# Output projection by pairs of units: two PSUM banks at a time, the attention's halves of both first, then the convolution's halves of both

## The chip, the cores and the metric

The kernel runs on 1 core of one Trainium2 chip. The time is device microseconds (us) of one execution of the whole program, taken from the runs of one kernel. A run of the hardware profiler gives, beside it, a span and a trace of every instruction. Engines are named as the profile does: PE is TensorE's matmul, PEld its weight load, DVE is VectorE, ACT is ScalarE, POOL is GpSimd, SP is SyncE, whose queue issues the DMAs. L213 is line 213 of the kernel; TensorE's clock has two levels, 1.2 and 2.4 GHz, which the profile gives as a granted share of 0.50 and 1.00.

## The reference

Two layers of a streaming encoder, all in fp32. A prompt of 1024 tokens and 8 samples of 16 tokens (128 together) pass through both layers; D_MODEL is 1024, the attention is 512 wide (8 heads of 64, 2 key and value heads), the convolution has 512 channels and 31 taps, the feed-forward is 4096 wide. Cut to what matters here:

```
def project(h, w_in, q_g, k_g, pos):
    q, k, v, a, b = jnp.split(h @ w_in, [...])
    ...                       # norm of q and k by head, partial rotary
    return q, k, v, a * jax.nn.sigmoid(b)

def conv_tail(u_ext, w, b, ln_g, ln_b):
    y = depthwise_conv31(u_ext, w) + b
    mu = mean(y); var = mean(square(y - mu))          # over the 512 channels
    return silu((y - mu) * rsqrt(var + EPS) * ln_g + ln_b)

def finish_layer(x, attn_o, conv_o, beta_a, beta_c, w_out, g2, w_up, w_down):
    x = x + concatenate([attn_o * beta_a, conv_o * beta_c]) @ w_out
    h = rms_norm(x, g2)
    return x + square(relu(h @ w_up)) @ w_down
```

`h @ w_in` starts from an RMS norm of x, and the attention is a sliding window over three chunks of 64 tokens with one sink logit for each head; the samples see their cached keys instead. The change touches the product with `w_out` alone.

## The kernel before, in words

**Tiling.** The 1152 tokens are three blocks (0, 1, 2) of 384 columns; the samples are the last 128 columns of block 2. Activations lie with the channels on the partitions, so a product takes a weight tile of 128 x 128 as the stationary operand and 384 columns as the moving one. An fp32 operand is kept as a rounded part and a remainder (fp32r), and a product takes three matmuls: rounded by rounded, rounded by remainder, remainder by rounded (L213, L214, L215 in `gemm`). One output tile of 128 channels over 1024 inputs, a *unit*, is 8 steps of three, 24 matmuls, into one PSUM bank.

**A weight's way.** `unit` (L195) makes two `half_unit`s of four steps each: SP issues a DMA of 256 KB into one of four buffers "raw", ACT rounds it (L205), POOL takes the remainder (L206) into one of six buffers "w". The remainder is what the third matmul of a step waits for.

**PSUM.** All products with 384 columns share three banks with the tag "g", which `pg` hands out: the input projection, the up and down projections, and `w_out`. Other banks are r (sums over channels and their spreading), c, m and s (attention). A bank is free for the next product when its result has been read, in `w_out` by DVE's addition into x (L688).

**`w_out`, L682 to L689.** For each of the 8 output tiles: a bank, a unit, whose steps 0 to 3 read the attention's result `ao` and 4 to 7 the convolution's `co`, the addition, and `unit_done` (L166), which moves the side lanes (attention, convolution, weight forms) on by a step at their rates and puts in feed-forward products of an earlier block.

**Where it is called.** `out(b)` in `run` completes the convolution's tail of block b (`tail_of`: mean, mean square at L242, the root as a power on POOL, its spreading over the partitions by PE at L248, the product with it at L663, then SiLU on ACT), loads x, calls `w_out`, and for blocks 0 and 1 the RMS norm ahead of the up projection (sum of squares L265 and L266, its root, products with it L276 and L278). It is called six times. In layer 0, block 0 comes without feed-forward products beside it, blocks 1 and 2 have them; in layer 1 all three have. Layer 1's block 0 has those of layer 0's block 2.

**What sets the order.** The program is written as a list and then set by a scheduler of the tile framework, which holds the written order as priorities and simulates the engines (`schedule_with_timeline_sim=True`, L1258). So each engine's queue follows its estimate of when operands are there, and the written order only in part; an edit in one place can move instructions elsewhere. A queue runs in its order: an instruction that waits holds all behind it.

Names in the rows: ao and co as above, hid a hidden tile of the feed-forward (L716 is the down projection, L718 its addition into x), c and u the convolution (L348, one tap of one tile of channels), pt the attention's transposed probabilities (L553 their remainder, L561 the product with the values), p and m the samples' (L612 scales them, L616 transposes them, L596 their scores), s small statistics, f and h the norm's output, vec and cst constants.

Of the kernel before, what the change touches and what calls it, by code (L numbers as in the profile page):

```python
# [11 lines left out]
ALU = mybir.AluOpType  # L12
# [8 lines left out]
KT = D // 128  # L21
UP = 30 + 256
SEG = CS + DEC_T
NS, NW, NRAW, NT, WK = 9, 6, 4, 8, 4
# [37 lines left out]
class Kernel:  # L62
# [619 lines left out]
    def w_out(self, l, x, ao, co):  # L682
        nc, a = self.nc, self.a
        h = lambda p, k: ao[:, p, k] if k < 4 else co[:, p, k - 4]
        for m in range(KT):
            ps, _ = self.pg()
            self.mark = self.gemm(ps, self.unit(a["w"][l, 14 + m]), h)
            nc.vector.tensor_tensor(out=x[:, m], in0=x[:, m], in1=ps, op=ALU.add)  # L688
            self.unit_done()  # L689


    def hidden(self, ps):
# [479 lines left out]
def _layout(i):  # L1172
# [12 lines left out]
    w = np.empty((DEPTH, 86, 128, 8, 128), np.float32)  # L1185
    w[:, :14] = tiles(w_in[:, :, cols])
    w[:, 14:22] = tiles(w_out)
    w[:, 22:54] = tiles(f("w_up"))
    w[:, 54:] = f("w_down").reshape(DEPTH, 8, 4, 128, 8, 128)[:, :, np.argsort(ROW)].transpose(0, 1, 3, 4, 2, 5).reshape(DEPTH, 32, 128, 8, 128)
# [72 lines left out]
```

## Time and profile before

| | |
|---|---|
| time, median of 3 runs | 2398.71 us (2397.44 to 2403.24) |
| profiled execution | 2401.53 us |
| its span | 2399.6 us |
| granted TensorE clock, mean | 0.991 |
| PE busy | 2319.6 us, 97% |
| PEld busy | 2257.2 us, 94% |
| DVE busy | 1652.4 us, 69% |
| POOL busy | 1533.8 us, 64% |
| ACT busy | 1270.9 us, 53% |
| DMA | 266.49 MB, 111 GB/s over the span |

The busy shares say which engine fills the span; they are means over stages with different limits. In the timeline a row is a run of like instructions of one engine: its start, its length, and in brackets the idle time of the engine just ahead of it with what ended it. Matmuls are pipelined and their ends modelled. The busy time of a matmul is the time it took, at whatever clock; the windows give the granted clock of a stretch beside it.

### The profile page before, as it was taken

Reading aid. Unit: us, or ns where it says so; the run is one execution under the profiler, and the core shown is the slowest. Engines: PE = TensorE matmul, PEld = TensorE weight load, DVE = VectorE, ACT = ScalarE, POOL = GpSimd, SP = SyncE. Lnnn points to the kernel's source line nnn. Section 1 sums busy time; section 2 is a strip of 40 time slices with the busy share of each in tenths; the row PEclk is TensorE's granted clock in tenths of the full one; section 3 lists DMA queues with packets and bytes.
Section 4 is the critical chain, followed back from the end, with each engine's and each line's share of the span. In section 5 each row is a group of like instructions: output and inputs, shape, how many; then the busy total and the mean of one; then the engine's idle time right before and its main releaser. Section 6 shows DMA issues by size and latency. Waiting matters only on the chain.

```text
span 2399.6 us, 38990 instructions
## 1 busy us (share of the span) xinstructions
PE 2319.6 (97%) x13822; PEld 2257.2 (94%) x13822; DVE 1652.4 (69%) x2997; ACT 1270.9 (53%) x2732; POOL 1533.8 (64%) x1371
## 2 busy tenths in 40 slices
PE   6899898999999999999999999999999999999999
PEld 6889898999999999999999999999999899999999
DVE  5999987996377777696687763699833877752222
ACT  5466655665335555644565476466443555544442
POOL 6875576666467666766956776856445766666662
PEclk9899899999999999999999999999999999999999
DMA  5322433333322122433333344423333122244432
GB/s 180 135 83 91 137 97 114 116 128 118 111 93 81 65 71 86 167 121 126 106 115 121 113 152 129 134 94 123 98 101 119 58 67 75 84 163 137 132 127 75
DMA packets 164259, 266.49 MB, mean 111 GB/s; under 512 B 24752, under 2 KB 55728, under 8 KB 164016
## 3 DMA queue, kind: packets, MB, share of 16 engines
q1 hardware_dynamic: 164064, 264.01, 33.6%
q8 instruction: 108, 1.77, 0.3%
q14 instruction: 87, 0.71, 0.1%
HBM read 250.19 MB, written 16.05 MB: 111 GB/s over the span
## 4 chain that ended last, share of the span: by engine, by line
PE 75%; DVE 18%; POOL 2%; DMA 2%; issue 2%; ACT 1%; SPq 0%; DVEq 0%; POOLq 0%; ACTq 0%
PE g L716 13%; PE g L213 13%; PE g L215 12%; PE g L214 12%; DVE c L348 6%; PE x L999 5%; PE x L919 4%; PE g L999 3%; PE g L919 2%; PE m L716 2%; PE r L716 2%; PE c L716 1%; POOL w L886 1%; DVE f L276 1%; DVE x L718 1%
## 5 line engine op out<-in xcount | busy, mean ns | idle before, releaser
L206 POOL TENSOR_TENSOR w<-raw,w 128x512 fp32r<-128x512 f32 x728 | 971.1, 1344 | 579.5 <-ACT w L205 562.9
L205 ACT CAST w<-raw 128x512 fp32r<-128x512 f32 x728 | 445.0, 619 | 452.0 <-PE g L716 127.3
L213 PE MATMUL g<-h,w 128*128 128x384 f32 x1696 | 577.4, 341 | 6.1 <-ACT h L277 3.5
L214 PE MATMUL g<-h,w 128*128 128x384 f32 x1696 | 574.9, 339 | 1.1 <-DVE h L278 1.1
L215 PE MATMUL g<-h,w 128*128 128x384 f32 x1696 | 575.4, 339 | 0.0
L348 DVE SCALAR_TENSOR_TENSOR c<-u,vec,c 128x384 f32<-128x384 f32 (+1 forms) x960 | 498.0, 519 | 18.6
L716 PE MATMUL g<-hid,w 128*128 128x384 f32 x2304 | 429.3, 340 | 6.7 <-DVE x L718 5.3
L716 PEld LDWEIGHTS g<-hid,w 128*128 128x128 f32 x2304 | 399.3, 189 | 15.1 <-DVE x L718 9.9
L213 PEld LDWEIGHTS g<-h,w 128*128 128x128 f32 x1696 | 322.2, 190 | 9.5 <-ACT h L277 4.3
L214 PEld LDWEIGHTS g<-h,w 128*128 128x128 f32 x1696 | 322.0, 190 | 2.9 <-DVE h L278 2.0
L215 PEld LDWEIGHTS g<-h,w 128*128 128x128 f32 x1696 | 321.8, 190 | 1.1 <-issue 0.3
L700 DVE TENSOR_TENSOR hid<-t,hid 128x384 fp32r<-128x384 f32 x128 | 106.4, 832 | 198.1 <-ACT hid L699 198.0
L886 POOL TENSOR_TENSOR w<-S,w 128x512 fp32r<-128x512 f32 x96 | 139.8, 1459 | 117.0 <-ACT w L885 116.8
L718 DVE TENSOR_TENSOR x<-x,g 128x384 f32<-128x384 f32 x240 | 129.8, 548 | 78.0 <-PE g L716 77.7
L697 ACT ACTIVATE t<-g 128x384 f32<-128x384 f32 x128 | 62.9, 492 | 144.8 <-PE g L215 143.8
L999 PE MATMUL x<-F,w 128*128 128x384 f32 x624 | 119.1, 336 | 2.9 <-DVE x L1002 2.0
L886 POOL TENSOR_TENSOR w<-raw,w 128x512 fp32r<-128x512 f32 x64 | 90.8, 1419 | 41.4 <-ACT w L885 40.1
L999 PEld LDWEIGHTS x<-F,w 128*128 128x128 f32 x624 | 109.4, 188 | 4.2 <-DVE x L1002 2.3
L999 PE MATMUL g<-F,w 128*128 128x384 f32 x528 | 108.2, 340 | 3.6 <-ACT F L808 1.5
L885 ACT CAST w<-S 128x512 fp32r<-128x512 f32 x96 | 59.7, 622 | 93.7 <-DVE S L872 48.4
L999 PEld LDWEIGHTS g<-F,w 128*128 128x128 f32 x528 | 92.6, 188 | 7.8 <-ACT F L808 2.7
L886 POOL TENSOR_TENSOR w<-A,w 128x512 fp32r<-128x512 f32 x64 | 87.0, 1364 | 17.8 <-ACT w L885 17.6
(231 smaller groups left out, 4005.6 us busy)
## 6 DMA issues: line engine op xcount, KB each, us to landing
raw<-in_w SPq DMA_DIRECT2D x792, 256.0 KB, 2.6
A<-in_w SPq DMA_DIRECT2D x64, 256.0 KB, 2.7
x<-in_x SPq DMA_DIRECT2D x24, 384.0 KB, 5.3
x<-xd SPq DMA_DIRECT2D x12, 384.0 KB, 5.4
kept<-x SPq DMA_DIRECT2D x4, 768.0 KB, 3.9
x<-kept SPq DMA_DIRECT2D x8, 384.0 KB, 4.3
xd<-x SPq DMA_DIRECT2D x4, 768.0 KB, 3.5
out_y<-x SPq DMA_DIRECT2D x4, 768.0 KB, 5.2
```

What stands on the lines that cost most here:

```text
L205: nc.scalar.copy(u[:, 0], raw)
L206: nc.gpsimd.tensor_tensor(out=u[:, 1], in0=raw, in1=u[:, 0].bitcast(F32), op=ALU.subtract)
L213: nc.tensor.matmul(ps, lhsT=u(0, k), rhs=h(0, k), start=k == 0, stop=False)
L214: nc.tensor.matmul(ps, lhsT=u(0, k), rhs=h(1, k), start=False, stop=False)
L215: self.pe = nc.tensor.matmul(ps, lhsT=u(1, k), rhs=h(0, k), start=False, stop=k == KT - 1)
L348: t = nc.vector.scalar_tensor_tensor(out=o, in0=src(k), scalar=w, in1=o, op0=ALU.mult, op1=ALU.add)
L700: nc.vector.tensor_tensor(out=hid[:, 1], in0=f, in1=hid[:, 0].bitcast(F32), op=ALU.subtract)
L716: self.pe = nc.tensor.matmul(ps, lhsT=u(p), rhs=hid[:, q], start=i == 0, stop=i == n - 1)
L718: nc.vector.tensor_tensor(out=x[:, m], in0=x[:, m], in1=ps, op=ALU.add)
L886: nc.gpsimd.tensor_tensor(out=u[:, 1], in0=f[n], in1=u[:, 0].bitcast(F32), op=ALU.subtract)
L919: nc.tensor.matmul(ps, lhsT=u[:, p, k], rhs=H[h](q, k), start=start and k == 0 and i == 0, stop=k == 3 and i == 2, skip_group_check=True)
L999: nc.tensor.matmul(o, lhsT=u[:, p, 2 * i + j], rhs=F(j, hn)[:, q], start=start and n == 0, stop=n == 5, skip_group_check=True)
```

## The change

The loop over 8 output tiles becomes a loop over 4 pairs. A pair takes two banks at once; then four half units follow: attention's of the first tile, attention's of the second, convolution's of the first, convolution's of the second. Each bank's accumulation starts with its first attention matmul and stops with its last convolution matmul, so it stays open while the other bank's half is done. Both additions and both `unit_done` come at the end of the pair. `gemm` is written out in the loop; the matmuls of the projection are now at L692, their additions at L694, and lines behind are six higher than before (L716 becomes L722).

```
--- before.py
+++ after.py
@@ -682,11 +682,17 @@
     def w_out(self, l, x, ao, co):
         nc, a = self.nc, self.a
         h = lambda p, k: ao[:, p, k] if k < 4 else co[:, p, k - 4]
-        for m in range(KT):
-            ps, _ = self.pg()
-            self.mark = self.gemm(ps, self.unit(a["w"][l, 14 + m]), h)
-            nc.vector.tensor_tensor(out=x[:, m], in0=x[:, m], in1=ps, op=ALU.add)
-            self.unit_done()
+        for m0 in range(0, KT, 2):
+            ps = [self.pg()[0] for _ in range(2)]
+            for part in range(2):
+                for i in range(2):
+                    u = self.half_unit(a["w"][l, 14 + m0 + i][:, part * WK:part * WK + WK])
+                    for k in range(WK):
+                        for j, (p, q) in enumerate(((0, 0), (0, 1), (1, 0))):
+                            self.mark = self.pe = nc.tensor.matmul(ps[i], lhsT=u[:, p, k], rhs=h(q, part * WK + k), start=part + k + j == 0, stop=part == 1 and k == WK - 1 and j == 2)
+            for i in range(2):
+                nc.vector.tensor_tensor(out=x[:, m0 + i], in0=x[:, m0 + i], in1=ps[i], op=ALU.add)
+                self.unit_done()
 
 
     def hidden(self, ps):
```

The scheduler sets all queues anew, and the places where they differ begin in the second pair of layer 0's first projection. Three of them follow.

PE, layer 0, ahead of the convolution's halves of block 1 (g is a bank, hid a down projection, ao a unit's attention half, co a convolution half, L248 the spreading of the convolution tail's root, L450 and L407 are statistics and turns of queries and keys). Before:

```order
L213 MATMUL g_4275<-ao_1778,w_4277 128x384
L214 MATMUL g_4275<-ao_1778,w_4277 128x384
L215 MATMUL g_4275<-ao_1778,w_4277 128x384
L248 MATMUL r_3919<-cst,s_3927 128x128 x3
L450 MATMUL r_3988<-cst,s_3783 64x128 x2
L407 MATMUL r_3999<-cst,t_3412 128x128
L213 MATMUL g_4030<-co_3941,w_4037 128x384
L213 MATMUL g_4117<-co_3941,w_4124 128x384
```

The first three are the last of 12 matmuls of the same attention half; ahead of those 12 stands the down projection g_4183. Now:

```order
L722 MATMUL g_4183<-hid_3565,w_4179 128x384 x3
L722 MATMUL g_4183<-hid_3671,w_4179 128x384 x3
L248 MATMUL r_3919<-cst,s_3927 128x128 x3
L692 MATMUL g_4275<-ao_1778,w_4278 128x384 x12
L450 MATMUL r_3988<-cst,s_3783 64x128 x2
L407 MATMUL r_3999<-cst,t_3412 128x128
L692 MATMUL g_4030<-co_3941,w_4067 128x384
```

L248 stood behind the 12 matmuls of the attention half, and stands ahead of them now.

DVE, layer 0, ahead of the first products of the RMS norm behind block 0's projection (L348 is a convolution step, L503, L565 and L567 belong to the attention). Before:

```order
L503 RECIPROCAL s_3050<-s_3050 128x4
L348 SCALAR_TENSOR_TENSOR c_3092<-u_1779,vec,c_3092 128x384 x2
L565 TENSOR_TENSOR og_2663<-m_2648,vec 128x256
L348 SCALAR_TENSOR_TENSOR c_3092<-u_1779,vec,c_3092 128x384
L567 TENSOR_TENSOR ao_1778<-og_2663,ao_1778 128x4x64
L276 SCALAR_TENSOR_TENSOR f_3250<-x_2764,vec,r_3231 128x384 x2
```

Now:

```order
L503 RECIPROCAL s_3085<-s_3085 128x4
L348 SCALAR_TENSOR_TENSOR c_3127<-u_1779,vec,c_3127 128x384
L565 TENSOR_TENSOR og_2663<-m_2648,vec 128x256
L348 SCALAR_TENSOR_TENSOR c_3127<-u_1779,vec,c_3127 128x384 x2
L567 TENSOR_TENSOR ao_1778<-og_2663,ao_1778 128x4x64
L348 SCALAR_TENSOR_TENSOR c_3127<-u_1779,vec,c_3127 128x384
L553 TENSOR_TENSOR pt_2874<-m_2873,pt_2874 128x512
L348 SCALAR_TENSOR_TENSOR c_3127<-u_1779,vec,c_3127 128x384 x2
L276 SCALAR_TENSOR_TENSOR f_3250<-x_2764,vec,r_3231 128x384 x2
```

A split of 512 columns (L553) came ahead of the norm's products. Counted from the first addition of squares of this norm to L276, the convolution steps are 27 in place of 25, the splits of 512 columns 3 in place of 2.

PE, layer 1, at the samples' first step (L596 scores, L616 transposes of the probabilities, g_18333 and g_18358 two down projections). Before:

```order
L716 MATMUL g_18314<-hid_18184,w_18310 128x384 x2
L596 MATMUL s_18248<-kc_17974,qb_18242 128x144 x6
L616 MATMUL m_18020<-cst,p_17999 128x128 x2
L616 MATMUL m_18020<-cst,p_18000 128x128 x2
L716 MATMUL g_18333<-hid_17968,w_18329 128x384 x3
L716 MATMUL g_18333<-hid_18088,w_18329 128x384 x3
```

Now:

```order
L722 MATMUL g_18314<-hid_18184,w_18310 128x384 x2
L596 MATMUL s_18248<-kc_17974,qb_18242 128x144 x6
L722 MATMUL g_18333<-hid_17968,w_18329 128x384 x3
L722 MATMUL g_18333<-hid_18088,w_18329 128x384 x3
L722 MATMUL g_18333<-hid_18135,w_18329 128x384 x3
L722 MATMUL g_18333<-hid_18184,w_18329 128x384 x3
L722 MATMUL g_18358<-hid_17968,w_18354 128x384 x3
L722 MATMUL g_18358<-hid_18088,w_18354 128x384 x3
L722 MATMUL g_18358<-hid_18135,w_18354 128x384 x3
L722 MATMUL g_18358<-hid_18184,w_18354 128x384 x3
L616 MATMUL m_18020<-cst,p_17999 128x128 x2
L616 MATMUL m_18020<-cst,p_18000 128x128 x2
```

Two down projections, 24 matmuls, came between the samples' scores and the transposes.

## Rows read from the trace of the kernel before

**Rows 1.** The page: span, then busy time, share and instructions of each engine.

```profile
span 2399.6 us, 38990 instructions
PE 2319.6 (97%) x13822; PEld 2257.2 (94%) x13822; DVE 1652.4 (69%) x2997; ACT 1270.9 (53%) x2732; POOL 1533.8 (64%) x1371
```

**Rows 2.** Windows: stretch, length, busy PE, PEld, DVE, ACT, POOL, clock, DMA, GB/s.

```profile
298.00:304.00 6.00, 5.99 (x19) 5.99 (x20) 6.00 (x11) 1.45 (x2) 0.69 (x1) 0.50 0.00 0
361.00:366.00 5.00, 3.04 (x25) 2.93 (x22) 3.05 (x7) 1.33 (x4) 5.00 (x5) 1.00 0.40 137
382.80:386.00 3.20, 3.20 (x10) 3.04 (x11) 3.16 (x8) 2.15 (x5) 0.97 (x1) 0.50 0.98 377
1651.00:1655.00 4.00, 2.88 (x10) 2.47 (x11) 4.00 (x9) 0.60 (x2) 3.21 (x4) 0.67 0.39 131
1800.00:1850.00 50.00, 50.00 (x289) 50.00 (x289) 22.10 (x41) 17.72 (x33) 27.34 (x22) 1.00 0.39 132
```

**Rows 3.** PE's timeline, 240 to 300: start, length, group, [idle before, releaser].

```profile
245.20 1.61 PE L561 MATMUL m<-pt,v 128*128 128x256 f32 x9 [2.12 <-DVE pt L553]
...
292.07 1.33 PE L561 MATMUL m<-pt,v 128*128 128x256 f32 x9 [0.93 <-DVE pt L553]
...
294.85 0.90 PE L248 MATMUL r<-cst,s 128*128 128x128 f32 x3 [1.44 <-POOL s L236]
...
298.01 1.01 PE L213 MATMUL g<-h,w 128*128 128x384 f32 x2 [1.41 <-ACT h L277]
```

**Rows 4.** PE's timeline, 362 to 384.

```profile
363.58 2.37 PE L716 MATMUL g<-hid,w 128*128 128x384 f32 x12 [1.97 <-DVE x L718]
...
375.23 0.41 PE L213 MATMUL g<-ao,w 128*128 128x384 f32 x1 [0.74 <-ACT w L205]
...
377.41 0.49 PE L248 MATMUL r<-cst,s 128*128 128x128 f32 x3
...
379.74 0.44 PE L450 MATMUL r<-cst,s 128*64 128x128 f32 x4 [1.85 <-DVE u L663]
...
382.78 1.33 PE L213 MATMUL g<-co,w 128*128 128x384 f32 x3 [1.88 <-ACT co L641]
```

**Rows 5.** PE's timeline in layer 1, beside its second projection.

```profile
1651.29 0.44 PE L616 MATMUL m<-cst,p 128*128 128x128 f32 x2 [0.90 <-DVE p L612]
...
1652.56 0.69 PE L616 MATMUL m<-cst,p 128*128 128x128 f32 x2 [0.83 <-DVE p L612]
```

**Rows 6.** DVE's timeline, 289 to 292.

```profile
289.10 0.68 DVE L553 TENSOR_TENSOR pt<-m,pt 128x512 fp32r<-128x512 f32 x1
...
290.34 1.28 DVE L348 SCALAR_TENSOR_TENSOR c<-u,vec,c 128x384 f32<-128x384 f32 x2
```

**Rows 7.** POOL's timeline, 290 to 295.

```profile
290.45 0.86 POOL L231 TENSOR_TENSOR s<-s,half 128x3 f32<-128x3 f32 x1
...
292.66 1.32 POOL L231 TENSOR_TENSOR s<-s,half 128x6 f32<-128x6 f32 x1
...
294.61 0.19 POOL L236 TENSOR_TENSOR s<-s,s 128x3 f32<-128x3 f32 x1
```

**Rows 8.** POOL's timeline, 368 to 375.

```profile
368.80 0.85 POOL L231 TENSOR_TENSOR s<-s,half 128x3 f32<-128x3 f32 x1
...
372.27 1.29 POOL L206 TENSOR_TENSOR w<-raw,w 128x512 fp32r<-128x512 f32 x1 [0.21 <-ACT w L205]
...
374.69 0.19 POOL L236 TENSOR_TENSOR s<-s,s 128x3 f32<-128x3 f32 x1
```

**Rows 9.** DVE's timeline, 371 to 378.

```profile
371.52 0.56 DVE L718 TENSOR_TENSOR x<-x,g 128x384 f32<-128x384 f32 x1 [4.13 <-PE g L716]
...
377.93 1.75 DVE L663 TENSOR_TENSOR u<-u,r 128x1536 f32<-128x1536 f32 x1 [2.85 <-PE r L248]
```

**Rows 10.** DVE's timeline in layer 1, ahead of the samples' transposes.

```profile
1650.40 2.10 DVE L612 TENSOR_SCALAR p<-p,s 128x256 f32<-128x256 f32 x2
```

**Rows 11.** Waits of PE: engine, line, waited for: us in total, times, longest.

```profile
PE g L716 <- DVE x L718: 5.3, 6, 2.0
```

## The prediction

> **What bounds the kernel now.** The page comes first: TensorE (PE) is busy for 2319.6 of 2399.6 us [rows 1]. So a change of order pays only where PE stands still, or runs at a lower clock. At the full clock one matmul of 384 columns costs PE 173 ns: 289 of them fill 50 us [rows 2]. Next I read PE's timeline for rows with an idle time in brackets, and then the granted clock around each. The reader is to see that idle time in the out projections is scarce. The four first places are: before the convolution's halves of block 0 in layer 0, where the longest wait is 2.12 us, and after block 0's projection, 0.93 + 1.44 + 1.41 = 3.78 us in all [rows 3]; before the convolution's halves of block 1, 1.97 + 0.74 + 1.85 + 1.88 us [rows 4]; and in layer 1 beside its second projection 0.90 + 0.83 us [rows 5]. The clock stands at 0.50 (1.2 GHz) in 298 to 304 and in 382.8 to 386, and is 0.67 on average in 1651 to 1655, each time after PE has idled [rows 2].
>
> **What the change does to the counts: nothing.** Each of the 48 units keeps 24 matmuls, two weight loads, two casts, two splits and one addition; no instruction is added or removed. What moves is the order, and with it two things: two of the three PSUM banks "g" belong to a projection at a time, and SP, ACT and POOL bring four half units as attention, attention, convolution, convolution. The scheduler then sets every queue anew, so I go by the places where the two orders differ.
>
> **Block 0's projection, layer 0: 0 at its start.** The change's plain promise, attention halves to run while the convolution is late, is already kept before: PE has the attention's halves of three units ahead of the wait at 245.20 [rows 3], one in each bank, and in the changed order also three. Up to there all queues hold the same work; the convolution's last product and its pass through ACT end the wait, as now. 0 us.
>
> **After it: +2.0 us.** The up projection at 298.01 waits for the RMS norm of this block [rows 3]. On VectorE (DVE) two more convolution steps and one split of 512 columns now stand ahead of the norm's products (counted from the first addition of squares to L276): a pair of steps takes 1.28 us, the split 0.68 us [rows 6], together 1.96 us. DVE has no idle row here, so they count in full. On POOL the key's power, 1.32 us, goes ahead of the norm's, where it stood in its midst [rows 7]. The chain on POOL starts later by DVE's shift and ends with both interleaved, so I do not add the 1.32 again: +2.0, bounds 0 (DVE has work in hand to give back) and 1.96 + 1.32 = 3.3.
>
> **Block 1's projection, layer 0: -2.8 us.** Here PE waits at 382.78 for the convolution tail, whose chain is mean square (L242), root on POOL, spreading it (L248), product (L663), SiLU on ACT. The root starts at 368.80 and its last step is over at 374.69 + 0.19 = 374.9 [rows 8], but L248 runs at 377.41 [rows 4]: in PE's queue it stands behind a unit's 12 attention matmuls, which themselves begin after a wait of 0.74. In the changed order L248 stands directly behind the last down projection, and the 12 follow it. So it can go earlier by 0.74 + 12 x 0.173 = 2.8 us; by POOL's end alone, 2.5. POOL also has one weight split less (1.29 [rows 8]) between the root's steps. The 12 matmuls then fill part of the wait that L248 to L663 causes (1.85). L663 begins at 377.93, right behind L248, and takes 1.75 [rows 9]; all behind it moves with it. The wait of 1.97 does not go: then the first down projection waited for an addition, now it follows the last query's statistics out of their bank, which DVE reads at about the same time. -2.8; bounds 0 (another link of the chain is late) and -(0.74 + 1.85 + 1.88) = -4.5.
>
> **The clock behind it: -0.8 us.** Ten matmuls fill the 3.2 us at 0.50 [rows 2], half of that is lost, 1.6. With the wait shorter, the drop may go or stay; I take half. Bounds -1.6 and +1.6 (such a drop elsewhere).
>
> **Layer 1, first sample step: -3.0 us.** PE's transposes L616 wait twice for DVE's scaled probabilities, ready at 1650.40 + 2.10 = 1652.50 [rows 5, 10]. In the changed order two down projections, 24 matmuls or 4.2 us, stand between the scores and these transposes; PE would reach them near 1654.6. DVE has two additions of at most 0.56 [rows 9] put ahead of the scaling, ready by 1653.6, still in time. So 0.90 + 0.83 go, and with the idle time the dip: (1 - 0.67) x 4 = 1.3 us. -3.0, bounds 0 and -3.0.
>
> **Elsewhere 0**: in the other projections PE is full in both orders, the feed-forward products of the background hide what moves on SP, ACT and POOL; without that cover a weight load and its cast would show.
>
> Sum: +2.0 - 2.8 - 0.8 - 3.0 = -4.6 us. Against the profiled execution's 2401.5 us (2.0 more than its span) this gives 2396.9. The median of the runs shown is 2398.7, so I forecast 2394.1. By the bounds: -9.1 to +4.9, that is 2389.6 to 2403.6.
>
> **Rivals.** *Banks run short (slower).* Five of the six projections have feed-forward products beside them, 20 pairs. If at each pair a down projection finds the only free bank still waiting for its addition, PE loses at least one addition, 0.56 us [rows 9]: 11.2 us. With +2.0 and -2.8 that is 2409. It decides from 13 pairs on (7.3 us). For it: the wait of 1.97 is of this kind [rows 4], and four down projections and a unit share one bank in the changed order ahead of block 1's convolution halves. Against it: all waits of L716 for such additions are 5.3 us in six places [rows 11], though units and down projections share the banks before too, and in most pairs both units of a pair follow each other without a product between, so the third bank is idle rather than short. Where PE did wait 1.97, the clock of 361 to 366 stayed at 1.00 (2.4 GHz) [rows 2]. The Trainium skill, "TensorE: Matmul & The Clock Gate", section "A second HAM failure mode: psum-queue depth-cycling", says that a kernel that cycles through its PSUM banks idles often enough between groups for the clock to swing between its two levels. By that rule this rival would cost more than its additions; the stretch just named does not bear it out.
>
> *The drops go (faster).* DVE gives its 2.0 back before the up projection, block 1's chain takes the whole -4.5, and both clock losses go: -4.5 - 1.6 - 3.0 = -9.1, 2389.6. For it: DVE's convolution steps done earlier are not to be done later, and PE-bound stretches follow. Against: it needs every step at its good end.
>
> *The orders are a wash.* The scheduler places instructions by its own times; where the chip differs, another link takes over. With +2.0, nothing at block 1, and only the 1.7 us of waits gone in layer 1, the time is 2399. For it: the change does not do at block 0 what it is made for, since that order was there already. Against: L248's 2.5 us behind its operand is plain in the trace.
>
> **Chances.** Forecast 0.46, wash 0.20, drops go 0.24, banks short 0.10. About 0.3% (7.2 us) can be told from no change. Faster: all of the third but its weaker part, 0.21, and the good end of the forecast, 0.06, makes 0.27. Slower: the bank rival, 0.10. The rest, 0.63, is the same. The range takes the bounds a little further on both sides, for orders that I weighed only by their waits: 2388 to 2405, which leaves out the bank rival and the far end of the fast one. The likeliest case's own range is 2390 to 2403.
>
> **What would show it.** In the changed profile: a longer wait ahead of the first up projection behind block 0's projection (about 3.3 us at near 300 for 1.41); L248 of the convolution tail right behind a down projection and near 374 to 377, and block 1's first convolution half 1 us earlier than 382.78 (2.0 late, 2.8 early); no idle row at the first L616 of layer 1 and clock 1.00 there. Many short waits of L716 or L692 for additions would make the bank rival right. Idle time at new places in 400 to 690 or 1380 to 1720 would make the forecast wrong.

## The result, and the profile after

The changed kernel takes 2416.18 us (median of 4 runs, 2414.68 to 2421.46), the kernel before in the same comparison 2399.13 us (2397.44 to 2403.24, 4 runs): ratio 1.0072, 95% interval 1.0059 to 1.0085. I had forecast 2394.1, with 2405 as the upper end: 2416, 17 us slower, is outside the range.

The page of the changed kernel, span and busy times:

```profile
span 2414.1 us, 38981 instructions
PE 2324.5 (96%) x13822; PEld 2260.7 (94%) x13822; DVE 1672.1 (69%) x2997; ACT 1271.4 (53%) x2732; POOL 1525.7 (63%) x1371
```

Against [rows 1] the span is 14.5 us longer. PE makes the same 13822 matmuls in 4.9 us more, so some of them ran at the lower clock; the other 9.6 us are idle time of PE. To find the place, I set the two timelines side by side at landmarks that both have: the mean square of block 0's convolution tail near 230 us, the first up projection behind block 0 near 298, the first product of layer 0's paired feed-forward that goes from its hidden tiles F into a bank x, near 750 (paired feed-forward: blocks 0 and 1 together, behind block 2's projection; below this landmark is "the first product with F", though a few products from F into banks g come up to 11 us earlier in both kernels), and the end.

| stretch | before | after |
|---|---|---|
| start to mean square | 231.5 | 228.3 |
| mean square to first up projection | 66.6 | 69.9 |
| up projection to first product with F | 452.7 | 464.9 |
| from there to the last matmul | 1644.9 | 1646.9 |

The first row is no effect of the change: up to there all queues are the same, and six kernels whose block 0 is as before reach this point between 228.1 and 231.7 us. Most of the loss lies in the third row, which holds the projections of blocks 1 and 2. The windows of the kernel before over that row (stretch, length, busy PE, PEld, DVE, ACT, POOL, clock, DMA, GB/s; 560 only parts the two projections):

```profile
298.00:382.80 84.80, 77.79 (x479) 73.36 (x479) 60.34 (x110) 39.71 (x76) 60.52 (x74) 0.96 0.30 97
382.80:560.00 177.20, 176.02 (x1077) 171.50 (x1078) 164.12 (x389) 109.01 (x291) 105.43 (x97) 0.99 0.38 122
560.00:708.50 148.50, 146.86 (x837) 144.09 (x836) 78.87 (x132) 62.28 (x115) 86.02 (x72) 1.00 0.33 106
708.50:750.70 42.20, 36.26 (x198) 33.69 (x197) 33.12 (x43) 25.70 (x53) 29.33 (x20) 1.00 0.26 86
```

and of the kernel after:

```profile
298.20:381.50 83.30, 78.00 (x476) 73.67 (x476) 62.74 (x107) 39.22 (x75) 59.59 (x74) 0.95 0.33 99
381.50:560.00 178.50, 172.39 (x1052) 167.45 (x1053) 165.95 (x383) 108.15 (x288) 105.42 (x98) 0.99 0.38 118
560.00:712.60 152.60, 149.17 (x844) 147.03 (x843) 78.57 (x135) 63.95 (x119) 87.52 (x73) 0.99 0.34 106
712.60:763.10 50.50, 42.66 (x215) 39.62 (x214) 35.40 (x46) 25.30 (x54) 28.40 (x20) 0.93 0.24 79
```

Length less busy PE is idle time: 7.0, 1.2, 1.6 and 5.9, together 15.8 us before; 5.3, 6.1, 3.4 and 7.8, together 22.7 after. The lower clock costs (1 - clock) x length; summed over windows of 5 us it is 4.7 us before and 10.6 after. So of the 12.3 us (464.94 less 452.66) some 6.9 are waits, and nearly as much, 5.9, is the slower clock (idle time at the lower clock counts in both). The last window also holds 17 more matmuls, 2.9 us, that stood ahead of it before.

PE's timeline of the changed kernel at these places (start, length, group, [idle before, releaser]):

```profile
298.20 1.01 PE L213 MATMUL g<-h,w 128*128 128x384 f32 x2 [2.41 <-ACT h L277]
...
362.27 0.38 PE L442 MATMUL g<-cst,t 128*128 128x2 f32 x2 [2.10 <-DVE s L439]
...
375.50 0.49 PE L248 MATMUL r<-cst,s 128*128 128x128 f32 x3
...
381.54 0.79 PE L692 MATMUL g<-co,w 128*128 128x384 f32 x3 [1.71 <-ACT co L641]
383.75 4.96 PE L692 MATMUL g<-co,w 128*128 128x384 f32 x18 [1.43 <-DVE co L642]
...
487.26 4.95 PE L722 MATMUL g<-hid,w 128*128 128x384 f32 x27 [1.52 <-DVE x L724]
...
531.08 5.48 PE L722 MATMUL g<-hid,w 128*128 128x384 f32 x30 [1.77 <-DVE x L724]
...
692.38 0.79 PE L722 MATMUL g<-hid,w 128*128 128x384 f32 x3 [1.72 <-POOL w L206]
694.23 2.08 PE L722 MATMUL g<-hid,w 128*128 128x384 f32 x7 [1.07 <-DVE x L724]
```

and the windows around the waits, where the clock is read in the column ahead of the last two:

```profile
363.70:367.20 3.50, 3.50 (x15) 3.50 (x14) 0.56 (x1) 0.58 (x1) 3.25 (x5) 0.51 0.22 74
381.60:387.00 5.40, 3.97 (x14) 3.66 (x15) 5.31 (x8) 2.09 (x5) 2.45 (x2) 0.75 0.63 230
384.20:387.70 3.50, 3.50 (x13) 3.50 (x13) 2.71 (x6) 0.00 (x0) 0.89 (x1) 0.51 0.26 85
692.00:698.00 6.00, 4.55 (x16) 4.24 (x17) 6.00 (x12) 1.88 (x4) 6.00 (x7) 0.74 0.30 101
720.00:726.00 6.00, 4.05 (x14) 3.81 (x14) 5.76 (x7) 2.18 (x4) 3.89 (x3) 0.72 0.14 44
736.00:742.00 6.00, 2.68 (x15) 2.03 (x13) 6.00 (x8) 1.43 (x3) 3.81 (x3) 1.00 0.02 6
742.00:748.00 6.00, 6.00 (x26) 6.00 (x27) 3.90 (x7) 5.30 (x13) 5.08 (x4) 0.72 0.43 131
1667.00:1671.00 4.00, 4.00 (x24) 4.00 (x25) 4.00 (x6) 1.71 (x7) 4.00 (x5) 1.00 0.47 131
```

In 736 to 742 PE stands still for 3.3 of 6 us, and in the next 6 us it is busy throughout but makes 26 matmuls where the full clock has room for 35. Between 560 and 750 us the clock of before was 1.00 throughout, so the three drops, in 692 to 698, 720 to 726 and 742 to 748, are new. The last row answers to the dip in layer 1 [rows 2, 5]: PE is full there at 1.00.

### The profile page after: what moved, and what is told of

The parts are those of the page before. It is cut to its first block, busy times and chain, and to the rows that moved or that the text cites. A ratio compares the mean times of both kernels' runs of the same rounds, so it can differ in the third digit from the quotient of the medians.

```text
span 2414.1 us, 38981 instructions
## 1 busy us (share of the span) xinstructions
PE 2324.5 (96%) x13822; PEld 2260.7 (94%) x13822; DVE 1672.1 (69%) x2997; ACT 1271.4 (53%) x2732; POOL 1525.7 (63%) x1371
## 4 chain that ended last, share of the span: by engine, by line
PE 52%; DVE 6%; POOL 1%; issue 1%; DMA 1%; ACT 0%; DVEq 0%; POOLq 0%; ACTq 0%
PE g L722 9%; PE g L213 8%; PE g L214 8%; PE g L215 8%; PE g L692 4%; PE x L1005 3%; PE x L925 2%; PE m L722 2%; PE r L722 2%; PE g L1005 2%; PE c L722 1%; PE g L925 1%; DVE c L348 1%; PE s L526 1%; POOL w L892 1%
## 5 line engine op out<-in xcount | busy, mean ns | idle before, releaser
L206 POOL TENSOR_TENSOR w<-raw,w 128x512 fp32r<-128x512 f32 x728 | 967.4, 1339 | 582.4 <-ACT w L205 553.1
L348 DVE SCALAR_TENSOR_TENSOR c<-u,vec,c 128x384 f32<-128x384 f32 (+1 forms) x960 | 498.4, 519 | 19.2
L722 PE MATMUL g<-hid,w 128*128 128x384 f32 x2304 | 431.2, 341 | 10.2 <-DVE x L724 7.4
L722 PEld LDWEIGHTS g<-hid,w 128*128 128x128 f32 x2304 | 400.7, 189 | 18.4 <-DVE x L724 11.4
L692 PE MATMUL g<-co,w 128*128 128x384 f32 x576 | 111.9, 343 | 3.5 <-ACT co L641 2.1
L692 PE MATMUL g<-ao,w 128*128 128x384 f32 x576 | 108.7, 338 | 3.2 <-DVE x L694 2.5
```

The source lines that it names most:

```text
L206: nc.gpsimd.tensor_tensor(out=u[:, 1], in0=raw, in1=u[:, 0].bitcast(F32), op=ALU.subtract)
L348: t = nc.vector.scalar_tensor_tensor(out=o, in0=src(k), scalar=w, in1=o, op0=ALU.mult, op1=ALU.add)
L692: self.mark = self.pe = nc.tensor.matmul(ps[i], lhsT=u[:, p, k], rhs=h(q, part * WK + k), start=part + k + j == 0, stop=part == 1 and k == ...
L722: self.pe = nc.tensor.matmul(ps, lhsT=u(p), rhs=hid[:, q], start=i == 0, stop=i == n - 1)
```

## The experiments

Every ratio is to the kernel before on the same chip. Beside the ratio stands the time from the mean square near 230 us to the first product with F (519.2 us before, 534.8 in the full change), since it tells where a ratio comes from. These times are from one profiled execution of each kernel.

**The place: pairs in one block only.** The edit of the first four (`w_pairs` is the projection as changed, `w_out` as before):

```
-self.w_out(l, x[b], ao[b], co)
+(self.w_pairs if (l, b) == (0, 0) else self.w_out)(l, x[b], ao[b], co)   # e1; e2: (0, 1); e3: (0, 2); e4: l == 1
```

> Pairs only in layer 0's block 0, which has no feed-forward products beside it. Theory A (two held banks make the products beside the projection wait): no loss here, ratio 0.998 to 1.001. Theory B (the new order that the scheduler sets behind the place costs, wherever it is): up to half of the 17 us, ratio 1.002 to 1.004.

> Pairs only in layer 0's block 1. Theory A: about 4 to 6 us slower (the part between 380 and 560 us in the changed kernel's trace), ratio 1.002 to 1.0025. Theory B: any sign, within 0.996 to 1.004, and not the lag that stands in the full change's trace at this place.

> Pairs only in layer 0's block 2. Theory A: the largest part, about 10 us slower (between 595 and 760 us), ratio 1.004, lost at the projection's end and at the paired feed-forward behind it. Theory B: any sign, within 0.996 to 1.004.

> Pairs only in layer 1. The changed kernel's trace has no further lag behind 760 us, so by theory A and by my third step (the samples' waits go) 0 to 3 us faster: ratio 0.9985 to 1.000. Theory B: any sign, up to 1.004.

Measured: block 0 1.0022 (1.0013 to 1.0032), block 1 1.0020 (1.0006 to 1.0033), block 2 1.0034 (1.0023 to 1.0045), layer 1 0.9999 (0.9990 to 1.0007). The four excesses add to 0.75%, the full change has 0.72%. So the loss is in layer 0 and in all three of its projections, and not a scatter over the whole program. The stretches say the same: from up projection to F, 456.6 us with pairs in block 1 and 460.8 in block 2, 4.0 and 8.1 more than before. Theory A had no loss in block 0 and is wrong there. Layer 1 loses nothing, though its projections have feed-forward products beside them too; no run here shows why. Nor does it gain: the 0 to 3 us that I expected of e4 did not come.

**Block 0: the last pair by units.**

```
-for m0 in range(0, KT, 2):
+for m0 in range(0, KT - 2, 2):      # tiles 6 and 7 as before; in layer 0's block 0 only
```

> Pairs only in layer 0's block 0, its last two tiles by whole units as before. Theory E (both last additions come together, so the norm's last squares start late and the up projection 4.2 us late): ratio 0.999 to 1.001, and the stretch from the mean square at 230 to the up projection is 66.5 to 67.5 us in place of 70.9. Theory F (the bank wait inside the projection and the work that DVE has ahead): the stretch stays at 69 to 71 us, ratio 1.0015 to 1.003.

Measured 1.0019 (1.0009 to 1.0028); theory E falls. From the last convolution matmul to the up projection it is 16.1 us, as in the full change, 15.3 with the whole block in pairs, 13.4 before. The rest of the 70 us is not the change's: the time from the mean square to that last matmul is 53 to 54 us in some kernels and 55 to 57.5 in others, and the kernel with pairs in block 2 alone, whose block 0 is as before, is among the latter (55.3).

**Block 2: queue orders at the paired feed-forward.** With pairs in block 2, DVE's timeline there reads:

```profile
723.44 0.54 DVE L942 TENSOR_TENSOR t<-t,x 128x384 f32<-128x384 f32 x1
729.48 1.54 DVE L887 TENSOR_TENSOR S<-raw,A 128x512 f32<-128x512 f32 x1 [5.50 <-DMA A<-in_w]
730.94 0.55 DVE L942 TENSOR_TENSOR x<-t,x 128x384 f32<-128x384 f32 x1
```

and ACT's:

```profile
717.03 0.61 ACT L900 CAST w<-raw 128x512 fp32r<-128x512 f32 x1
723.55 0.62 ACT L900 CAST w<-S 128x512 fp32r<-128x512 f32 x1 [5.90 <-DVE S L887]
...
725.63 0.47 ACT L938 COPY t<-x 128x384 f32<-128x384 f32 x1
```

A weight sum that waits for its DMA stands ahead of an addition that PE's next products need, and a cast that waits for a sum ahead of a copy out of PSUM. Before, both stood the other way round. Four runs put them back: DVE's order, in block 2's pairs (e5) and in the full change (e6), then both orders (e9, e10). The edit in words:

```
+self.after(first_sum_of_third_quad, first_pair_addition, first_pair_split)     # DVE
+self.after(cast_of_weight_sum, copy_out_of_psum)                               # ACT, six casts; e9 and e10
```

> Pairs only in layer 0's block 2, and one thing put back: DVE's queue holds the third quad's first weight sum (which waits for a DMA) behind the additions of the feed-forward's first pair, where it stood before. Theory C (one instruction that waits for a DMA, ahead of work that PE needs): the 8.8 us between the first product with T and the first with F go back to the 42.1 us of the kernel before, ratio 0.9985 to 1.001. Theory D (the two down projections that are left behind the projection cost it): at most 2 to 3 us come back, ratio 1.0022 to 1.0032.

> The full change with the same one thing put back. If the three places in layer 0 add up and theory C holds: 1.0072 less 8.4 us of 2400, so ratio 1.0037, 1.0025 to 1.005. If the scheduler's scatter gives the time back or takes it elsewhere: anything from 1.002 to 1.008.

> Pairs only in layer 0's block 2, with the DVE order put back and ACT's too: the second copy out of PSUM at the first pair of the feed-forward stands ahead of the casts of weight sums, where it stood before (in the other kernel it stands behind four casts that wait for DVE's sums). Theory C2 (the two queue orders are the whole 8.8 us): the stretch from the first product with T to the first with F is 42 to 44 us in place of 50.9 and 48.6, ratio 0.9985 to 1.001. Theory D (what the projection leaves behind it costs): the stretch stays above 46 us, ratio 1.002 to 1.0035.

> The full change with both orders put back at that one place. Theory C2: the stretch is 42 to 44 us in place of 50.5, ratio 1.0025 to 1.0045. Theory D: above 46 us, ratio 1.0055 to 1.007.

Measured: 1.0037 (1.0024 to 1.0051), 1.0067 (1.0054 to 1.0079), 1.0029 (1.0019 to 1.0039), 1.0062 (1.0049 to 1.0074). The stretch from the first product of the paired feed-forward to the first with F (the expectations say "the first product with T", but the product at its start reads h) falls from 50.9 to 48.6 and 46.8 us in block 2's pairs, and from 50.5 to 46.6 in the full change, against 42.1 before; none of the ratios is told apart from that of the same kernel without the edit. The orders cost about 4 us there in the traces; theories C and C2, that they are the whole of it, fall.

**What in the pair costs: banks, additions, rounds.** A *round* is one `unit_done`: side steps and feed-forward. In e8, e11, e13 and e17 the units are whole; e12 is the change with a round between the halves. In words:

```
 e8   two banks; unit 0, unit 1; addition, round, addition, round
 e11  two banks; unit 0, addition, round; unit 1, addition, round
 e12  two banks; attention halves, round; convolution halves, additions, round
 e13  two banks; unit 0, addition, unit 1, addition; round, round
 e17  one bank at a time; unit, addition, unit, addition; round, round
```

> All projections by pairs of tiles with two banks taken at once and both additions at the end, but each unit whole: attention and convolution half of the first, then of the second. If taking two banks and bunching additions is what costs: ratio 1.005 to 1.008, like the full change. If splitting the halves is: ratio 0.999 to 1.002. DVE's queue has the weight sum ahead at the paired feed-forward here too, so by theory C at least 8 us there: not under 1.003.

> Two banks taken at once for a pair of tiles, but each unit whole, with its addition and its feed-forward and side steps right behind it as before. Theory G (bunching: two additions and two rounds of feed-forward at once): nothing of the loss is here, ratio 0.998 to 1.0015. Theory H (two of three banks held): block 1's stretch (from its first convolution half to block 2's) stays near 265 us and the paired feed-forward's near 50 us, ratio 1.004 to 1.007.

> The full change, but one of the two rounds of feed-forward and side steps of each pair is put behind the attention halves and one behind the convolution halves, so the work beside comes evenly. Theory G: block 1's stretch falls from 266 to 261 to 263 us and the time to a ratio of 1.002 to 1.005. Theory H: block 1's stretch stays at 265 to 267 us, ratio 1.006 to 1.008.

> Two banks at a time, units whole, each addition right behind its unit, but both rounds of feed-forward and side steps at the pair's end. Theory J (late additions: the first tile's bank waits for the second tile): as fast as before, 0.998 to 1.0015, block 1's stretch 260 to 262 us. Theory K (two rounds of work beside at once): as slow as with both additions at the end, 1.005 to 1.008, block 1's stretch 264 to 267.

> The kernel before, one bank and one whole unit at a time, with the rounds of feed-forward and side steps called in twos behind every second unit. Theory K (rounds in twos cost by themselves): ratio 1.004 to 1.007 and 463 to 467 us from the up projection at 298 to the first product with F, as with two banks and whole units (465.2). If it takes the two held banks as well: 0.999 to 1.002 and 452 to 456 us.

Measured: e8 1.0068 (1.0055 to 1.0082), e11 0.9997 (0.9988 to 1.0006), e12 1.0067 (1.0055 to 1.0080), e13 1.0058 (1.0046 to 1.0071), e17 1.0056 (1.0039 to 1.0072). From mean square to F: 535.1, 520.3, 532.7, 532.4, 534.9. Two banks taken at once cost nothing (e11). The place of the additions makes no difference that can be told. e8, e13 and e17 also have the same stretch lengths, 265.1 us from block 1's first convolution half to block 2's and 49.7 for the paired feed-forward up to F (260.5 and 42.1 before), with two banks or one. Calling the rounds in twos costs 0.56% with nothing else in the code changed (e17). It also puts the weights of two units one behind the other, ahead of both rounds; what of the two costs, this run does not tell. One round between the halves saves nothing (e12, whose block 1 stretch is 268.4), so the split costs too.

**What in the split costs.** e14 and e15 are the change with other ends of the pair, e16 is the kernel before with the change's order of weights alone.

```
 e14  two banks; attention halves; convolution half 0, addition, round; convolution half 1, addition, round
 e15  two banks; attention halves; convolution half 0, addition; convolution half 1, addition; round, round
 e16  four half units fetched as attention, attention, convolution, convolution; then
      one bank: unit 0, addition, round; one bank: unit 1, addition, round
```

> The full change, but addition and round of work beside stand right behind each tile's convolution half: attention halves of both, then convolution half, addition and round of the first, then of the second. Theories J and K: most of the loss is gone, what is left is the 2.7 us behind block 0's projection less 1.4 at block 1: 0.999 to 1.002. Theory L (the split into halves costs of itself, by the order of weights): 1.004 to 1.008.

> The full change with each addition right behind its tile's convolution half and both rounds of work beside at the pair's end. Theory J: 0.999 to 1.002. Theory K: 1.005 to 1.008. Theory L: 1.004 to 1.008, like the run with the rounds put behind each tile.

> The kernel before with nothing but the order of weights of the change: for each pair of tiles the four half units are fetched and split as attention, attention, convolution, convolution; the matmuls, banks, additions and rounds of work beside stay unit by unit. Theory L (the split costs by the order of weights): ratio 1.004 to 1.010, from the up projection at 298 to the first product with F 460 us or more in place of 453. If the split costs by its matmuls in PE's queue: 0.999 to 1.002 and 452 to 455 us.

Measured: e14 1.0111 (1.0096 to 1.0127), e15 1.0086 (1.0072 to 1.0099), e16 1.0087 (1.0072 to 1.0102); 542.7, 538.5 and 538.0 us from mean square to F. e14, which I had thought the best version of the change, is the slowest of all, above the ranges of all theories; why is open. Fetching the weights as the change does, attention's first and for both units ahead of the first one's round, costs as much as the whole change by itself (e16), with every matmul, bank, addition and round in the written place of before. No run has whole units' weights fetched for two units ahead and the rounds single, so the order of the halves and the fetching in twos are not told apart; the second is in e17 too. The waits of PE from block 1's projection to the paired feed-forward (us in total, times, longest) in the kernel before:

```profile
PE g L716 <- DVE x L718: 1.0, 3, 0.6
PE g L716 <- DVE x L688: 0.9, 1, 0.9
```

in e11:

```profile
PE g L721 <- DVE x L723: 1.0, 3, 0.6
PE g L721 <- DVE x L693: 0.9, 1, 0.9
```

in e17:

```profile
PE g L718 <- DVE x L720: 6.0, 5, 2.0
PE g L718 <- DVE x L688: 1.4, 1, 1.4
```

in e16:

```profile
PE x L925 <- DVE t L933: 4.3, 1, 4.3
PE g L722 <- DVE x L724: 3.5, 3, 2.2
PE g L722 <- POOL w L206: 3.1, 1, 3.1
```

and in the full change:

```profile
PE g L722 <- DVE x L724: 4.6, 4, 1.8
PE g L722 <- POOL w L206: 1.7, 1, 1.7
```

With rounds in twos the down projections wait longer for additions; with the weights in twos also for a weight's split on POOL and, in the paired feed-forward, PE waits for DVE (4.3 us at once). From up projection to F the idle time is 23.1 us in e17 and 26.0 in e16 (15.8 before), the clock's loss 13.1 and 15.1 (4.7 before). The two edits do not add: both are in the full change, at 0.72%. How either leads to each of these waits I have not shown.

## Why the prediction was wrong

- **Counts, and block 0's start:** right. From the mean square to the last convolution matmul 53.2 us before and 53.8 after; the attention's halves were ahead of the wait already. The wait of 2.12 us itself was misread: what ends it is the split of the attention's probabilities (L553 [rows 3]), and block 0's convolution halves then come without a wait of their own, in the kernel before at 248.26:

```profile
248.26 1.33 PE L213 MATMUL g<-co,w 128*128 128x384 f32 x3
```

- **After it, +2.0:** right, a little small. The up projection follows the last convolution matmul by 16.1 us in place of 13.4: +2.7.
- **Block 1's chain, -2.8:** half, and then lost again. L248 runs behind the down projection as the order shows, 77.3 us behind the first up projection in place of 79.4 [rows 3, 4], 2.1 us gained. The first convolution half comes only 1.4 us earlier: on ACT a weight's cast now stands ahead of the convolution's first cast (L641). Behind it PE stood again, 1.43 us for the convolution's remainders, which before came without a wait. They were late on DVE: the query's turn (L288), ahead of them in its queue, took 1.62 us where it took 0.56 before, and POOL's queue now has a weight's split just then. ACT, DVE and POOL in the changed kernel, and L288 in the kernel before:

```profile
380.36 0.60 ACT L205 CAST w<-raw 128x512 fp32r<-128x512 f32 x1
380.87 1.12 ACT L641 ACTIVATE co<-u,vec 128x384 fp32r<-128x384 f32 x2
```

```profile
381.55 1.62 DVE L288 TENSOR_TENSOR t<-t,t 128x384 f32<-128x384 f32 x1 [0.89 <-POOL t L287]
```

```profile
381.47 1.28 POOL L206 TENSOR_TENSOR w<-raw,w 128x512 fp32r<-128x512 f32 x1
```

```profile
382.61 0.56 DVE L288 TENSOR_TENSOR t<-t,t 128x384 f32<-128x384 f32 x1 [0.89 <-POOL t L287]
```

- **The clock there, -0.8:** wrong in sign. The drop behind the waits for the convolution stayed: 382.8 to 386 at 0.50 before [rows 2], 384.2 to 387.7 at 0.51 after. And a new one came ahead of it, 363.7 to 367.2 at 0.51, so that in 298 to 382 the loss is 3.8 us for 3.1.
- **Layer 1, -3.0:** the waits at L616 are gone as worked out, but that is not the change's. From the end of layer 0's last product from F into x to the first product of layer 1's paired feed-forward it is 918.4 us before and 916.1 after, and 914.2 to 914.3 in the kernels with pairs in one block of layer 0 alone (e1, e2, e3) and in e11. None of these has pairs of halves in layer 1, and in all of them the waits at L616 are gone too. With pairs in layer 1 alone (e4) the ratio is 0.9999 (0.9990 to 1.0007): no gain to be told. That the term fits is luck.
- **Elsewhere 0: the step that failed.** I wrote that in the other projections PE is full in both orders and the feed-forward hides what moves. It does not: from block 1's first convolution half to the first product with F it is 381.6 us in place of 367.9, +13.7. I had compared the orders at the places where PE idled before, and had not gone through the places where it did not. In its place the profiles show waits of PE and the lower clock there: idle time of 17.4 us in place of 8.8, and 6.8 us lost to the clock in place of 1.6, together the 13.7. The cover itself was moved: what fills PE between units is the rounds and what feeds them is the weights, and the change puts both in twos; rounds called in twos cost 0.56% (e17), weights fetched for two units at once 0.87% (e16). Why layer 1, which has the same cover, loses nothing is open.
- **The rivals.** "Banks run short" had the right sign, the right place and in part the right kind of wait: over the whole run the waits of L722 for additions went from 5.3 us in six places [rows 11] to 7.4 in seven, and the projection's own first matmuls now wait 2.5 us for additions in two places, for 0.7 in one before. The new ones are few and 0.9 to 1.8 us long, where I had priced 0.56 at each of twenty pairs. Other waits are for a weight's split (1.72 us at 692) and, in the paired feed-forward, for ACT, POOL and DVE. Its reason was wrong: two banks taken at once cost nothing (e11), and with one bank at a time the loss is there all the same (e16, e17). And it left out the clock. I had set aside the rule of the Trainium skill, "TensorE: Matmul & The Clock Gate", section "A second HAM failure mode: psum-queue depth-cycling", because the stretch of 361 to 366 kept 1.00 after a wait of 1.97 [rows 2]. That page of the Trainium skill tells of a kernel that idles often enough between its groups of matmuls for the clock to swing; here 5.9 of 12.3 us are lower clock, which agrees. One row was no evidence against it: the same wait of 1.97 us is in e11, and there the clock did fall.

```profile
359.00 2.33 PE L721 MATMUL g<-hid,w 128*128 128x384 f32 x7 [1.97 <-DVE x L723]
```

```profile
359.40:362.80 3.40, 3.40 (x14) 3.40 (x12) 0.23 (x1) 0.21 (x1) 2.79 (x3) 0.50 0.45 136
```

## What to carry to other kernels

When an engine is full because other work is put between its units, a change in how the units are grouped is first a change in that cover: go through the places where the engine does not idle and ask what fills them, and what feeds the filling, before pricing the places where it does. In block 0 a saving by "attention first, while the convolution is late" was already made by the scheduler, so the change could only move things there; of the ten kernels here that had the order of weights or of rounds changed in all projections every one was 0.56 to 1.11% slower, and the one that had neither (e11) was the same. Price a wait with the clock behind it, and not by one row: the same wait of 1.97 us left the clock at 1.00 in the kernel before and was followed by 3.4 us at 0.50 in e11.

## What the runs showed of the hardware

The same DVE operation took 0.56 or 1.62 us (L288, 128 x 384), another 0.94 or 1.92 (L265, 128 x 768). In the profile after, 15 of the 30 L288 of this shape took 1.10 us or more, and all 15 have a weight's split (L206) on POOL beside them, 14 of these begun earlier than L288; of the 11 that took at most 0.61 us, 3 have one, in two cases begun later. L288 starts 0.08 us behind the split at 381.47, and its 1.62 us are about what is left of the split, 1.20, and the 0.56 it takes alone. The Trainium skill, "SBUF — State Buffer", section "SBUF: two separate sides", says that a DVE operation with two SBUF inputs and a GpSimd operation that reads SBUF share one pair of ports, and the one that starts second is blocked until the other ends; these rows agree but for one short L288 behind a split, and no run of its own tested it. I had taken DVE's times as fixed. And the clock's drop can cost what the waits do: the waits of 1.72 and 1.07 us near 692 stand in a stretch of 6 us at 0.74, whose lower clock loses 1.6 us more.
